# Where the weight sums of a decoder step are formed, and from which half of the work an input's block sums come

## The chip, the cores and the metric

The kernel is one launch on one core of a Trainium2 chip. The metric is device time in microseconds (us) for the whole launch, which is also how every span below is given. In the text PE is TensorE, DVE is VectorE, ACT is ScalarE, POOL is GpSimd and SP is SyncE; POOL and SP issue the DMAs here.

## The reference

A decoder step with one layer of mixer A, one shared projection of keys and values, and one layer of mixer B, on 1024 prompt tokens and 8 decoded ones, all in fp32, with 2048 channels:

```python
def pool_layer(x, prefix, pos, w_in, w_grp, scale, w_out, g_ln, b_ln):
    z = x @ w_in                                  # 2048 -> 4096
    u, gate = z[..., :D_POOL], z[..., D_POOL:]
    d, new_state = multiscale_pool(u, prefix, pos)
    d = jnp.einsum('btgc,gce->btge', d.reshape(B, T, 4, 512), w_grp)
    d = d.reshape(B, T, D_POOL) * scale
    y = (d * jax.nn.silu(gate)) @ w_out           # 2048 -> 2048
    return layer_norm(ALPHA * x + y, g_ln, b_ln), new_state

def attn_layer(x, ..., w_in, sinks, w_out, g_ln, b_ln):
    z = x @ w_in                                  # 2048 -> 4096
    q = rope_partial(z[..., :D_ATTN].reshape(B, T, N_HEADS, HEAD_DIM), pos)
    gate = z[..., D_ATTN:]
    o = attn_core(q, kb, vb, q_pos, k_pos, sinks).reshape(B, T, D_ATTN)
    y = (o * jax.nn.silu(gate)) @ w_out           # 2048 -> 2048
    return layer_norm(ALPHA * x + y, g_ln, b_ln)
```

`attn_core` is attention over a sliding window of 128 keys, with a sink per head.

## The kernel before, in words

**Stages.** The tokens are cut into chunk 0 (512) and chunk 1 (520, with the decoded tokens). Four matrix products (`wia`, `woa`, `wib`, `wob`) run one after the other, each for both chunks: ai0, ai1, ao0, ao1, bi0, bi1, bo0, bo1. These are the eight stages; the sixth is bi1, the seventh bo0 and the eighth bo1. bi also holds the attention, bo the last layer norm.

**Products.** Each matrix product is done by Strassen's scheme in Winograd's form: for each pair of output blocks (pairs 0 to 7 of a stage of 2048 outputs), seven block products in place of eight. They need sums of weight blocks and sums of input blocks. Every operand is split into a rounded part `hi` and a rest `lo`, so that a product is 24 matmuls (L687 hi·hi, L688 hi·lo, L689 lo·hi), some 2.8 us together. The products are counted from the start of the program; that count is the clock of the schedule (`self.i`). At the start of each product the program writes the weight loads that belong up to 7 products ahead (SP), the ACT cast of `hi` (L508) of 4 ahead, and the DVE subtraction for `lo` (L523) of 3 ahead. Every engine works in the order in which the source writes its instructions: an instruction that waits holds up all behind it on its engine.

**Sums of weights.** For `wob` they are formed in two ways. For most pairs `sum_gen` forms them ahead, in stages before bo0: one of four parts of a pair is loaded to a slot (two DMAs), added by DVE (L456 on 128x512, L460 and L461 on 128x256) and stored to DRAM by POOL (L462); bo0 and bo1 load the finished sums. It runs when the flag `on` is set and more than 5 slots are free. For pairs in `LATE` the sums are formed in bo0 itself, when they are first needed (`first_pair`: four DVE adds of 128x1024, L352, and four stores by POOL a pair, L354), and bo1 loads them.

**Sums of inputs.** `t_ops` makes the sums of an input's blocks: four DVE operations of 128x256 or 128x260 (L898 to L901), and a POOL store of 512 or 520 KB (L902, to a tensor named `to` for the input of bo). For the eighth stage `t_gen` does that in bo0, in eight steps that load, sum and store two rows of blocks of `o`; it is one of the side generators, of which a step is taken at products. When bo1's inputs are wanted, what is left of it is run at once.

**Slots.** All these buffers are 54 slots of SBUF (`Mem`); slot 14 shows as m14 in the rows of order below. A whole slot (`full`) is the one that has been free longest; a slot that was freed with a store under way counts as freed ten releases later than it was. `half` hands out half of a slot: the other half of one already broken up, unless that was freed within the last 6 releases and more than 7 whole slots are free. Nothing but the order of release keeps an instruction off a slot whose store isn't done; if it gets one, it waits for that store.

Of the kernel before, what the change touches and what calls it, by code (L numbers as in the profile page):

```python
# [69 lines left out]
    (6, 3), (7, 2), (7, 1), (6, 4), (7, 3), (7, 4), (4, 5), (4, 6), (5, 5), (5, 6), (6, 5), (6, 6), (7, 5), (7, 6),  # L70
)

LATE = (2, 3)
FORM = (0, 1)
X_KEEP = 5
X_AGE = 3
# [63 lines left out]
class Mem:  # L140
# [22 lines left out]
    def half(self, n=TMAX):  # L163
        fits = lambda i: i < NWIDE or n <= 512
        part = [
            (a if b is None else b, i) for i, (a, b) in enumerate(self.f) if (a is None) != (b is None) and fits(i)
        ]
        if part and min(part)[0] > self.clock - 6 and len(self.whole()) > 7:
            part = []
        i = min(part)[1] if part else min((i for i in self.whole() if fits(i)), key=lambda i: max(self.f[i]))  # L170
        h = 0 if self.f[i][0] is not None else 1
        if not part:
            self.new(i)
        self.f[i][h] = None
        w = TMAX if i < NWIDE else 512
        return Slot(self, i, h, self.t[i][:, h * w : (h + 1) * w])
# [15 lines left out]
class Kern:  # L192
# [187 lines left out]
    def build_stream(self):  # L380
        io = self.io
        w = []
        for kind, c, part in PHASES:
# [33 lines left out]
            else:  # L417
                name = "woa" if kind == "ao" else "wob"
                if (kind, c, part) != PHASES[-1]:
                    prs = [self.next_pair(name, q) for q in range(8)]  # L420
                    if (kind, c) == ("bo", 0):
                        for q in LATE:
                            prs[q] = self.first_pair(name, q)
# [10 lines left out]
    def sum_gen(self, name):  # L434


        W = 256
        qs = [q for q in range(8) if name != "wob" or q not in LATE]
        parts = [(q, slice(W * h, W * h + W)) for q in qs for h in range(4)]
# [144 lines left out]
    def both(self, c, P, Q):  # L584

        runs = [self.seven(c, z0, z1, {6: done}, own=own) for (z0, z1, done), own in (
            (P, self.psW), (Q, self.psW if self.wide else self.psO)
        )]
        for idx in ORDERL:
            for run in runs:  # L590
                run(idx)

    def pair(self, c, z0, z1, done, c11=None):

        run = self.seven(c, z0, z1, {6: done}, c11)
        for idx in ORDER7:
            run(idx)
# [304 lines left out]
        nc.gpsimd.dma_start(dst[:, kp], t)  # L902
        s.free(True)

    def t_gen(self, key):
        T = CHUNKS[key[1]][1]
        s = {}

        def load(kp):
            s[kp] = self.mem.full(2 * T)  # L910
            self.nc.sync.dma_start(s[kp].v(2, T), self.act[key][:, 2 * kp : 2 * kp + 2, :])

        load(0)
        yield
        for kp in range(9):
            if kp < 7:
                load(kp + 1)
            if kp:
                v = s[kp - 1].v(2, T)
                self.t_ops(v[:, 0], v[:, 1], self.Td[key], kp - 1, T // 2)  # L920
                s.pop(kp - 1).free()
            yield


    def j_steps(self, T, a, b, box, *free):
# [1357 lines left out]
    def run(self):  # L2283
        io = self.io
        self.build_stream()
        self.needs, self.pe, self.summed, self.hurry = [], {}, {}, None
        self.sg, self.qs, self.ao = {}, {}, {}
        self.last = self.turn = self.lock = False
        self.need = {}
        self.shared = False  # L2290
        self.strassen = False
        self.start()

        def add(key, gen):
            self.needs.append((key, gen))
            self.side.append(gen)

        acc, before = {}, False
        for n, (kind, c, part) in enumerate(PHASES):
            self.c, self.ph = c, kind + str(c)  # L2300
            self.strassen = (kind, c, part) not in PLAIN
            self.shared = False
            self.fresh = c == 1 and before and self.strassen
            before = c == 0 and self.strassen
            nxt = n + 1 if n + 1 < len(PHASES) else None
            self.every, self.room = 3, SIDE_KEEP
            if n == 0 or (kind, c) == ("bi", 0) and self.wide:
                self.use_four(kind == "ai")
            elif (kind, c) == ("bo", 0):
                self.at(18, lambda: self.use_four(True))  # L2310

            self.lock = (kind, c) in LOCKED
            self.need = {
                (idx, g): self.i + (2 * n + g - 1 if self.lock else n)
                for n, idx in enumerate(ORDERL if self.lock else ORDER7) for g in range(2)
            } if self.strassen else {}
            self.turn = not self.lock
            self.at(7, lambda: setattr(self, "turn", False))
            self.at(13, lambda: setattr(self, "lock", False))
            if n == 0:  # L2320
                self.at(10, lambda: self.x_begin(1))
                self.at(10, lambda: setattr(self, "turn", True))
            elif (kind, c) == ("ai", 0):
                add(("x", 1, False), self.t_gen(("x", 1)))
                self.room = 99
            elif (kind, c) == ("ai", 1):
                add(("g", 0, False), self.t_gen(("g", 0)))
                self.summed["woa"] = 0
                add("woa", self.sum_gen("woa"))
                self.every = 1.7  # L2330
            elif (kind, c) == ("ao", 0):
                self.every = 2
                self.at(1, lambda: self.nc.sync.dma_start(self.cst[:, K_MP:], io["mask"]))
            elif (kind, c) == ("ao", 1):
                gen = self.ln_gen(0, *acc[0], C_GA, C_BA, self.act["h", 0], self.Td["h", 0])
                self.at(3, lambda gen=gen: add(("h", 0, True), gen))
                self.every = 1.5
            elif (kind, c) == ("bi", 0) and not self.strassen:
                self.summed["wob"] = 0
                self.extra = self.sum_gen("wob")  # L2340
                for k in (4, 5):
                    self.at(k, lambda k=k: setattr(self, "on", k == 4))
                add(("h", 1, False), self.ln_gen(1, *acc[1], C_GA, C_BA, self.act["h", 1], self.Td.get(("h", 1))))

                for k in range(14):
                    self.at(2 * k + 5, lambda: self.side and self.lastO < self.i - 1 and self.side_step())
                self.every, self.room = 1, -20
            elif (kind, c) == ("bi", 1):
                self.at(8, lambda: setattr(self, "on", True))
                self.every, self.room = 1, 0  # L2350
            elif (kind, c) == ("bo", 0):
                self.at(23, lambda: setattr(self, "ahead", (7, 4, 3)))
                self.at(18, lambda: add(("o", 1, False), self.t_gen(("o", 1))))
                self.at(16, lambda: [s.free() for s in self.kv])
                self.rt.free()
            elif (kind, c) == ("bo", 1):
                gen = self.ln_gen(0, *acc[0], C_GB, C_BB, io["y0"], None)
                self.at(3, lambda gen=gen: add("y", gen))
                self.every, self.room = 1.5, 3
            if kind == "ai":  # L2360
                self.phase_ai(c, range(*part), nxt)
            elif kind == "bi":
                self.phase_bi(c, range(*part), nxt)
            else:
                res = self.act["x" if kind == "ao" else "h", c]
                last = (C_GB, C_BB, io["y1"]) if nxt is None else None
                acc[c] = self.phase_out(c, res, nxt, last)
# [141 lines left out]
```

## Time and profile before

| | us |
|---|---|
| three runs | 2311.48, 2312.7, 2317.13 (median 2312.7) |
| profiled execution | 2315.52, of which its span is 2313.7 |
| PE busy | 2285.5 (99% of the span) |
| DVE busy | 1904.7 (82%) |
| ACT busy | 1388.2 (60%) |
| POOL busy | 218.4 (9%) |

In the profiled execution bi0's Strassen products run from about 1217 us to 1504, bi1 to 1941, bo0 to 2128 and bo1 to the end. A row of the waits gives engine, tile and line that waited, what it waited for, us in total, times and the longest. A row of the windows gives a stretch, its length, each engine's busy time with its count of instructions, the mean clock that TensorE was granted (1.00 is full), the DMA engines' busy share and GB/s. A row of the timeline gives start, duration, engine, line, operation, destination and sources with their shapes, and the idle time ahead of it with what ended it. POOL's rows are DMA issues for the most part; the last number of a row of DMA issues is the median us from issue to landing.

### The profile page before, as it was taken

The page shows a single profiled execution, that of the slowest core. Times are in us where ns is not written, and L with a number is a line of the kernel's source. Part 1 is how long each engine was busy: PE and PEld are TensorE (multiplying, and loading weights), DVE is VectorE, ACT ScalarE, POOL GpSimd, SP SyncE. Part 2 cuts the span into 40 slices and gives each one's busy share as a digit, 9 for nine tenths or more (in the row PEclk, how much of TensorE's full clock was granted, in tenths as well). Part 3 has the DMA queues.
Part 4 walks back from the last instruction along what each step waited for, and adds up shares of the span by engine and source line. Part 5 has one row for each costly group of instructions (what it writes and reads, how often), then busy time and mean ns, then how long its engine had stood idle before and what let it go on. Part 6 is the DMA issues. An engine that isn't in the chain of part 4 may idle for free. (4 is left out here: it accounts for less than half of the span.)

```text
span 2313.7 us, 50523 instructions
## 1 busy us (share of the span) xinstructions
PE 2285.5 (99%) x20353; PEld 2214.5 (96%) x20353; DVE 1904.7 (82%) x2413; ACT 1388.2 (60%) x2551; POOL 218.4 (9%) x399
## 2 busy tenths in 40 slices
PE   9999999999999999999999999999999999899998
PEld 8999999999999999999889999999999999899998
DVE  8888889877878878988868888899776777788997
ACT  5544446444546556555567676785676678556665
POOL 0111110010000000000111111100010100010001
PEclk9999999999999999999999999999999999999999
DMA  7779679988889989999777767777776779699894
GB/s 259 266 263 316 228 249 330 314 305 301 301 305 322 338 286 331 320 385 343 236 249 238 243 225 251 268 264 234 242 247 224 250 238 315 210 359 363 297 333 150
DMA packets 252028, 647.77 MB, mean 280 GB/s; under 512 B 27504, under 2 KB 112528, under 8 KB 251792
## 3 DMA queue, kind: packets, MB, share of 16 engines
q1 hardware_dynamic: 208640, 490.20, 63.2%
q0 software_dynamic: 43152, 154.34, 17.3%
q8 instruction: 159, 2.61, 0.5%
q14 instruction: 77, 0.63, 0.1%
HBM read 467.21 MB, written 177.23 MB: 279 GB/s over the span
## 5 line engine op out<-in xcount | busy, mean ns | idle before, releaser
L687 PE MATMUL pD<-m,m 128*128 128x260 f32 (+1 forms) x5088 | 1443.6, 284 | 4.9 <-ACT pD L626 2.2
L689 PE MATMUL pD<-m,m 128*128 128x260 f32 (+1 forms) x5088 | 1436.2, 282 | 6.0 <-DVE m L523 5.7
L688 PE MATMUL pD<-m,m 128*128 128x260 f32 (+1 forms) x5088 | 1436.5, 282 | 0.0
L687 PEld LDWEIGHTS pD<-m,m 128*128 128x128 f32 x5088 | 960.7, 189 | 14.8 <-issue 7.2
L689 PEld LDWEIGHTS pD<-m,m 128*128 128x128 f32 x5088 | 961.4, 189 | 8.0 <-DVE m L523 8.0
L688 PEld LDWEIGHTS pD<-m,m 128*128 128x128 f32 x5088 | 960.8, 189 | 0.5
L523 DVE TENSOR_TENSOR m<-m,m 128x1024 fp32r<-128x1024 f32 x690 | 833.4, 1218 | 94.6 <-ACT m L508 32.2
L508 ACT CAST m<-m 128x1024 fp32r<-128x1024 f32 x690 | 720.6, 1049 | 231.6 <-DVE m L352 118.5
L352 DVE TENSOR_TENSOR m<-m,m 128x1024 f32<-128x1024 f32 x136 | 166.2, 1222 | 15.1 <-DMA m<-in_wia 10.4
L850 DVE TENSOR_TENSOR m<-m,m 128x1024 fp32r<-128x1024 f32 (+1 forms) x118 | 144.0, 1225 | 4.4 <-ACT m L841 3.8
L841 ACT CAST m<-m 128x1024 fp32r<-128x1024 f32 (+1 forms) x118 | 123.4, 1053 | 4.5 <-DMA m<-in_x 2.4
L648 DVE TENSOR_TENSOR m<-pD,m 128x260 f32<-128x260 f32 (+1 forms) x92 | 39.0, 424 | 101.4 <-ACT pD L647 95.3
L660 ACT COPY m<-pD 128x260 f32<-128x260 f32 (+1 forms) x88 | 32.8, 372 | 122.4 <-PE pD L689 121.8
L1935 ACT ACTIVATE m<-m,sm 128x128 f32<-128x128 f32 x256 | 99.3, 392 | 0.0
L632 ACT COPY m<-pD 128x260 f32<-128x260 f32 (+1 forms) x90 | 33.6, 373 | 97.8 <-PE pD L689 93.1
L1184 PE MATMUL pD<-m,m 128*128 128x260 f32 (+1 forms) x528 | 91.5, 323 | 0.0
L715 PE MATMUL pD<-m,m 128*128 128x512 f32 x224 | 89.0, 397 | 0.0
L635 ACT COPY m<-pD 128x260 f32<-128x260 f32 (+1 forms) x92 | 34.4, 374 | 90.8 <-PE pD L689 90.7
L717 PE MATMUL pD<-m,m 128*128 128x512 f32 x224 | 88.2, 394 | 0.0
L716 PE MATMUL pD<-m,m 128*128 128x512 f32 x224 | 88.2, 394 | 0.0
L1184 PEld LDWEIGHTS pD<-m,m 128*128 128x128 f32 x528 | 79.4, 188 | 8.2
L1948 ACT ACTIVATE m<-m,sm 128x128 f32<-128x128 f32 x256 | 81.9, 393 | 2.7 <-DVE sm L1943 2.5
(259 smaller groups left out, 2082.4 us busy)
## 6 DMA issues: line engine op xcount, KB each, us to landing
m<-in_wib SPq DMA_DIRECT2D x132, 512.0 KB
m<-in_wia SPq DMA_DIRECT2D x128, 512.0 KB
m<-swoa SPq DMA_DIRECT2D x64, 512.0 KB
swia<-m POOLq DMA_DIRECT2D x56, 512.0 KB, 4.6
m<-swia SPq DMA_DIRECT2D x56, 512.0 KB
m<-swob SPq DMA_DIRECT2D x56, 512.0 KB
m<-in_wob SPq DMA_DIRECT2D x52, 512.0 KB
m<-in_woa SPq DMA_DIRECT2D x48, 512.0 KB
```

What stands on the lines that cost most here:

```text
L352: self.nc.vector.tensor_add(s[out].a[:, :1024], s[x].a[:, :1024], s[y].a[:, :1024])
L508: self.nc.scalar.copy(hi.r[:, :1024], self.stream[self.cast].src().a[:, :1024])
L523: self.nc.vector.tensor_sub(lo.r[:, :1024], s.src().a[:, :1024], hi.a[:, :1024])
L687: nc.tensor.matmul(ps[:, :TH], wh[:, s], h, start=new and k == 0, stop=False, skip_group_check=on)
L688: nc.tensor.matmul(ps[:, :TH], wh[:, s], l, start=False, stop=False, skip_group_check=on)
L689: nc.tensor.matmul(ps[:, :TH], wl[:, s], h, start=False, stop=k == 7, skip_group_check=on)
L715: nc.tensor.matmul(ps[:], wh[:, s], h, start=par == 0 and k == 0, stop=False)
L716: nc.tensor.matmul(ps[:], wh[:, s], l, start=False, stop=False)
L841: self.nc.scalar.copy(h.r[:, :n], s.a[:, :n])
L850: self.nc.vector.tensor_sub(l.r[:, :n], s.a[:, :n], h.a[:, :n])
L1184: nc.tensor.matmul(ps[:, : cs.stop - cs.start], ws[:, s], d[:, cs], start=f0 and k == 0, stop=l0 and k == 3,)
L1935: nc.scalar.activation(x["s3"][:, i, :], x["s3"][:, i, :], AF.Exp, bias=nm[:, i : i + 1], scale=0.125, accum_out=rs[:, i : i + 1],)
```

## The change

Three things. `LATE` is empty, so that the sums of `wob` pairs 2 and 3 are formed by `sum_gen` too; for that `on` is set in bi0 as well, from its product 20 to 74. `t_gen` takes a range of steps: the first four rows of the eighth stage's input sums are made in bi1 (from its product 94), the other four in bo0. `half` breaks up a whole slot when more than 3 are free, where 7 were needed.

```diff
-LATE = (2, 3)
+LATE = ()
...
-        if part and min(part)[0] > self.clock - 6 and len(self.whole()) > 7:
+        if part and min(part)[0] > self.clock - 6 and len(self.whole()) > 3:
             part = []
...
-    def t_gen(self, key):
+    def t_gen(self, key, a=0, b=8):
...
-        load(0)
+        load(a)
         yield
-        for kp in range(9):
-            if kp < 7:
+        for kp in range(a, b + 1):
+            if kp < b - 1:
                 load(kp + 1)
-            if kp:
+            if kp > a:
...
             yield
+            if b < 8:
+                yield
+                yield
...
+            elif (kind, c) == ("bi", 0):
+                self.at(20, lambda: setattr(self, "on", True))
+                self.at(74, lambda: setattr(self, "on", False))
             elif (kind, c) == ("bi", 1):
+                self.at(94, lambda: add(("o", 1, False), self.t_gen(("o", 1), 0, 4)))
                 self.at(8, lambda: setattr(self, "on", True))
                 self.every, self.room = 1, 0
             elif (kind, c) == ("bo", 0):
                 self.at(23, lambda: setattr(self, "ahead", (7, 4, 3)))
-                self.at(18, lambda: add(("o", 1, False), self.t_gen(("o", 1))))
+                self.at(18, lambda: add(("o", 1, False), self.t_gen(("o", 1), 4)))
```

In the program as written out, bi0's products 422 to 476 hold ten parts of weight sums that were not there (30 DVE adds, 10 POOL stores, 20 SP loads), and between them 2 to 5 whole slots are free where 4 to 7 were. bi1 holds as many parts as before, of other pairs, and sixteen operations of `t_ops`. bo0 has lost eight adds of L352 with their eight POOL stores, and half of `t_gen`; pairs 2 and 3 load seven blocks each there and no longer five. Lines behind `t_gen` are 3 higher than before (L929 is now L932, L1986 is L1989).

The first place is on DVE, in bi0, where `t_ops` makes one row of the sums of bo0's input (in the trace of before at 1341 us). Before, the four operations fill slot m2, and the next `lo` goes to slot m21:

```order
L1986 SCALAR_TENSOR_TENSOR m50_1799_15736<-pO_281_15969,m14_1733_14883 128x512
L898 TENSOR_TENSOR m2_1823_16059<-m50_1799_15736 128x256
L899 TENSOR_TENSOR m2_1823_16059<-m50_1799_15736 128x256
L900 TENSOR_TENSOR m2_1823_16059<-m50_1799_15736,m2_1823_16059 128x256
L901 TENSOR_TENSOR m2_1823_16059<-m50_1799_15736,m2_1823_16059 128x256
L523 TENSOR_TENSOR m21_1828_16080<-m33_1801_15748,m1_1822_16028 128x1024
```

The same place now:

```order
L1989 SCALAR_TENSOR_TENSOR m42_1803_15754<-pO_281_15994,m45_1733_14883 128x512
L898 TENSOR_TENSOR m2_1828_16084<-m42_1803_15754 128x256
L899 TENSOR_TENSOR m2_1828_16084<-m42_1803_15754 128x256
L900 TENSOR_TENSOR m2_1828_16084<-m42_1803_15754,m2_1828_16084 128x256
L901 TENSOR_TENSOR m2_1828_16084<-m42_1803_15754,m2_1828_16084 128x256
L456 TENSOR_TENSOR m25_1817_15924<-m25_1817_15924 128x512
L523 TENSOR_TENSOR m2_1834_16107<-m14_1805_15766,m33_1827_16053 128x1024
```

The first add of a weight sum (L456) has come in, and the `lo` now writes into m2, the slot that POOL has just begun to store.

The second place is on DVE in bo0 (in the trace of before from 1991 us on): L929 adds up parts of the layer norm's sums into a half slot, and two lines later stand the last steps of the decoded tokens' attention (L2096 to L2098), which PE waits for. Before:

```order
L1986 SCALAR_TENSOR_TENSOR m23_2554_24310<-pS_215_13092,m31_2531_24123 128x512
L2085 COPY m23_2554_24310<-pS_215_13092 128x128
L2086 TENSOR_REDUCE sm_476_24311<-m23_2554_24310 128x1
L2087 SCALAR_TENSOR_TENSOR sm_476_24311<-sm_476_24311,prm_75 128x1
L2088 TENSOR_TENSOR sm_477_24312<-prm_75,sm_476_24311 128x1
L2089 TENSOR_SCALAR sm_476_24311<-sm_476_24311 128x1
L1344 SCALAR_TENSOR_TENSOR m39_2574_24464<-m42_2552_24305,m39_2574_24464 128x1024
L523 TENSOR_TENSOR m27_2634_24975<-m11_2621_24815,m26_2632_24929 128x1024
L929 TENSOR_TENSOR m23_2554_24310<-m39_2574_24464 128x512
```

The same place now:

```order
L1989 SCALAR_TENSOR_TENSOR m15_2582_24410<-pS_215_13092,m43_2559_24220 128x512
L2088 COPY m15_2582_24410<-pS_215_13092 128x128
L2089 TENSOR_REDUCE sm_476_24411<-m15_2582_24410 128x1
L2090 SCALAR_TENSOR_TENSOR sm_476_24411<-sm_476_24411,prm_75 128x1
L2091 TENSOR_TENSOR sm_477_24412<-prm_75,sm_476_24411 128x1
L2092 TENSOR_SCALAR sm_476_24411<-sm_476_24411 128x1
L1347 SCALAR_TENSOR_TENSOR m25_2602_24564<-m40_2580_24405,m25_2602_24564 128x1024
L523 TENSOR_TENSOR m32_2663_25071<-m52_2648_24913,m2_2660_25027 128x1024
L932 TENSOR_TENSOR m23_2665_25114<-m25_2602_24564 128x512
```

Before, L929 wrote into m23, a slot that L1986 had just filled in part with a block of `o` for POOL to store. Now L932 writes into a whole slot that has been free for long, not into m15.

## The prediction

> **What bounds the kernel now.** I read the head of the page first, then PE's waits over the span, then the stages that the change touches.
>
> ```profile
> PE 2285.5 (99%) x20353; PEld 2214.5 (96%) x20353; DVE 1904.7 (82%) x2413; ACT 1388.2 (60%) x2551; POOL 218.4 (9%) x399
> ```
>
> ```profile
> PE pD L689 <- DVE m L523: 5.7, 8, 2.2
> PE pS L2102 <- DVE m L2098: 5.3, 1, 5.3
> PE pD L687 <- ACT pD L626: 2.2, 2, 1.3
> PE pD L687 <- ACT m L660: 1.5, 2, 1.1
> ```
>
> PE is busy all but 28 us of 2313.7, and the change takes no matmul away. So it can win only where PE waits or runs at a lower clock, and can lose wherever DVE, ACT or a transfer comes late at a product. The two largest waits are for DVE. Most of them are in bo0:
>
> ```profile
> PE pS L2102 <- DVE m L2098: 5.3, 1, 5.3
> PE pD L689 <- DVE m L523: 2.5, 2, 2.2
> PE pD L687 <- ACT m L660: 1.5, 2, 1.1
> ```
>
> ```profile
> 1998.00:2009.00 11.00, 5.72 (x32) 5.52 (x30) 7.57 (x10) 3.23 (x5) 0.53 (x1) 0.69 0.32 112
> 2090.00:2094.00 4.00, 1.77 (x15) 1.57 (x14) 4.00 (x5) 1.24 (x2) 0.53 (x1) 1.00 1.04 405
> 2094.00:2098.00 4.00, 4.00 (x23) 4.00 (x22) 3.91 (x4) 3.40 (x6) 0.53 (x1) 0.57 1.05 408
> ```
>
> The first three rows are PE's waits between 1941 and 2128 us, the others windows. In 11 us from 1998, PE is busy 5.72 and the clock granted is 0.69; from 2090 it is idle 2.23 us, and the 4 us behind that run at 0.57. A wait costs more than its own length.
>
> **bo0: what the change removes.** DVE's timeline says why PE waited:
>
> ```profile
> 1994.27 1.22 DVE L523 TENSOR_TENSOR m<-m,m 128x1024 fp32r<-128x1024 f32 x1
> 2000.39 0.69 DVE L929 TENSOR_TENSOR m<-m 128x512 f32<-128x512 f32 x1 [4.91 <-DMA o<-m]
> ...
> 2088.73 0.43 DVE L898 TENSOR_TENSOR m<-m 128x260 f32<-128x260 f32 x1 [2.44 <-DMA m<-o]
> ```
>
> L929 waited 4.91 us for the store out of the slot that it was to write, with the attention steps L2096 to L2098 behind it. It now gets a slot long free, so this wait goes. The second wait is the rest of `t_gen`, run in one go when bo1's inputs are wanted: its L898 waited 2.44 us for a load of `o`. With half of the rows already made in bi1, the generator is done before that point, so this goes too. The 1.5 us for L660 stood behind ACT casts that waited for the L352 adds of pairs 2 and 3, and these are gone. In sum, against the profiled execution:
>
> - 1998 to 2009: idle 11.00 − 5.72 = 5.3, and for the clock up to 0.31 × 11 = 3.4; less if only PE's busy 5.72 us are counted as slowed (taken: 2.9).
> - 2090 to 2098: idle 2.2, clock 0.43 × 4 = 1.7.
> - L660: 1.5.
>
> That is 13.6 us. What could be late next is the load: pairs 2 and 3 load seven blocks and no longer five (2 MB more in all), and the DMA share is 1.04 around 2090. But POOL's eight stores of 512 KB (4 MB) leave the same stretch, and a part of `t_gen`'s loads and stores with them. I put the new lateness at 0, and keep 0 to 6 us.
>
> **bi1.** As many parts of sums are made as before, and 16 operations of `t_ops` come in, 16 × 0.43 = 6.9 us of DVE by this row:
>
> ```profile
> L901 DVE TENSOR_TENSOR m<-m,m x56: 424/428/432, 87.2 to 2089.9; 128x260 f32<-128x260 f32 x32, 128x256 f32<-128x256 f32 x24
> ...
> 1504.00:1941.00 437.00, 435.60 (x4756) 425.38 (x4756) 331.57 (x456) 302.12 (x708) 38.35 (x60) 1.00 0.75 246
> ```
>
> DVE has 437 − 332 = 105 us to spare there, so that is covered; without the cover it would be the 6.9. PE is idle 1.4 us in the stage, and later waits for loads may add a little: +0.5, between −1 and +4.
>
> **bi0: what the change adds.** This decides. The stretch that gets ten parts of sums, products 422 to 476, lies between 1291 and 1474 us:
>
> ```profile
> 1291.00:1474.00 183.00, 183.00 (x2072) 178.72 (x2072) 156.49 (x189) 130.17 (x320) 28.92 (x55) 1.00 0.68 237
> ...
> L456 DVE TENSOR_TENSOR m<-m x56: 653/684/691, 442.7 to 1900.3; 128x512 f32<-128x512 f32 x56
> L460 DVE TENSOR_TENSOR m<-m x56: 374/424/428, 443.4 to 1902.0; 128x256 f32<-128x256 f32 x56
> L461 DVE TENSOR_TENSOR m<-m x56: 424/426/428, 443.9 to 1902.5; 128x256 f32<-128x256 f32 x56
> ```
>
> PE never waits there. DVE is idle for 183 − 156.5 = 26.5 us. Ten parts take 10 × (0.68 + 0.42 + 0.43) = 15.3 us, some 14 because successive operations overlap a little. By itself that would fit. But the parts also hold slots, which leaves 2 to 5 free, and the one free longest is then often the one just given to POOL to store. In the order of the changed kernel, `lo` (L523) goes to such a slot six times between products 438 and 476: three times a slot of `t_ops` (m2, m14, m11), directly behind it or with one L456 between, and three times a slot of a weight sum (m25, m43, m2), one to five operations behind the store. Each L523 must wait until that store has landed, and with it all that DVE does next: other `lo`, the sums that ACT casts, the evacuation of PSUM. The trace of before shows such waits, and what stores take in bi0 and bi1:
>
> ```profile
> DVE m L929 <- DMA o<-m: 4.9, 1, 4.9
> DVE m L523 <- DMA swob<-m: 3.1, 1, 3.1
> ```
>
> ```profile
> swib<-m POOLq DMA_DIRECT2D x37, 512.0 KB, 3.2
> ...
> to<-m POOLq DMA_DIRECT2D x5, 512.0 KB, 6.7
> ...
> swob<-m POOLq DMA_DIRECT2D x23, 512.0 KB, 5.5
> ```
>
> A store of `to` took a median 6.7 us from issue to landing and one of `swob` 5.5; `swib`, whole slots without a stride, 3.2. With 0.5 us until POOL issues, a `lo` directly behind `t_ops` waits about 7 us, one behind L456 some 6, and those behind a weight sum 5.5 + 0.5 less the DVE work in between: 3.6, 1.7 and 4.8. Together 7 + 7 + 6 + 3.6 + 1.7 + 4.8 = 30 us.
>
> Why this reaches PE is seen at one such place. Before, there is no wait:
>
> ```profile
> 1341.83 0.42 DVE L901 TENSOR_TENSOR m<-m,m 128x256 f32<-128x256 f32 x1
> 1342.17 1.22 DVE L523 TENSOR_TENSOR m<-m,m 128x1024 fp32r<-128x1024 f32 x1
> ...
> 1346.41 1.23 DVE L523 TENSOR_TENSOR m<-m,m 128x1024 fp32r<-128x1024 f32 x1
> ```
>
> ```profile
> 1349.30 0.28 PE L689 MATMUL pD<-m,m 128*128 128x256 f32 x1
> ...
> 1352.13 0.28 PE L689 MATMUL pD<-m,m 128*128 128x256 f32 x1
> ```
>
> The `lo` that ends at 1343.39 is first used at 1349.30, 5.9 us later, the next (1347.64) at 1352.13, 4.5 later. That is all the lead DVE has. A wait of 6 us with an L456 ahead of it and two more adds of sums behind it (0.68 + 0.85) takes 7.5: the second of the two is then about 3 us late, and what is late on DVE stays so until it has idle time, of which there is 26.5 / 183 = 0.14 us in each us. Walked through the queue like this, the six places give PE waits of 5, 2, 4, 3, 6 and 2 us, 22 in all. A rougher count agrees: DVE is asked for 30 + 14 = 44 us more where it has 26.5, so at least 17.5 are left over. I take 20, and 3 more for clock, as waits of 2.2 and 5.3 us cost 1.7 and some 3 in the rows above. The lower bound goes by the `swib` row: if every store landed in 3.2 us, the six waits fall by 3 × 3.5 + 3 × 2.3 = 17 to some 13, the demand to 27, and DVE would just keep up: 0. The upper bound counts no idle time, only the lead of 4.5 twice: 30 + 14 − 9 = 35. Twenty is nearest to the rows of the same stores (6.7 and 5.5), so I keep those.
>
> The Trainium skill has a rule on these stores: in "DMA: Bandwidth & Descriptors", section "Anatomy of one DMA — SWDGE (gpsimd) path", a DMA of this path takes about 2.0 us and its bytes over 436 GB/s, which is 3.2 us for 512 KB, an estimate by that page. The `swib` row agrees with it and the `to` and `swob` rows don't, at 6.7 and 5.5 us; by the page's figure the loss in bi0 would be about none, which is the first rival below.
>
> The Trainium skill also says, in "TensorE: Matmul & The Clock Gate", section "HAM oscillation — how this bites in real kernels", that PE gaps of over some 3.4 us lower the clock. The window behind the 2.2 us gap, 0.57 for 4 us, shows that here a shorter one can do it as well; by the page only two or three of the six waits would cost clock.
>
> ACT and the queues: SP issues 20 more loads in bi0 and POOL ten more stores of 0.7 us issue time, with POOL busy 28.9 of 183 us, and DMA share 0.68. That adds 10 × 1 MB in 183 us to the row's 237 GB/s, about 57 more; the rows of bo0 show 405 GB/s, so I count it as hidden.
>
> **Sum.** −13.6 + 0.5 + 20 + 3 = +9.9 us. The profiled execution took 2315.5 (span 2313.7 and 1.8 around it), 2.8 above the median of 2312.7. Against the profile that is 2325.4; against the median 2322.6. I forecast 2322 on the median's scale.
>
> **The rivals.**
>
> - *Stores land early, or DVE catches up in its idle time* (faster). For it: the `swib` row of 3.2 us, the 26.5 us of idle time, and a DMA share of 0.68. The point that decides is the wait at `t_ops`: under about 4 us, the lead of 4.5 covers it. Then only bo0's gain is left: 2312.7 − 13.6 + 0.5 ≈ 2300. Against it: five stores of `to` in this stage at a median of 6.7. Chance 0.15.
> - *The two sides cancel* (no change). If the six waits hit singly, each with its lead restored, the loss in bi0 is 13 to 15 us: 2312 to 2316. For it: the places are some 10 to 28 us apart. Chance 0.2.
> - *The waits feed on each other* (slower). ACT's casts then come late too and PE falls to half clock after each gap: +31 in bi0 in place of 23, about 2331. For it: the clock rows. Chance 0.12.
> - *bo0's gain doesn't come*, since the two more blocks a pair arrive late in a stage where the DMA share reaches 1.04 (the change doesn't do what it says): 2312.7 + 23.5 ≈ 2336. Against it: 4 MB of stores leave. Chance 0.05.
>
> **How the numbers follow.** My forecast, 2316 to 2328 by itself, has 0.48. A measurement of this kernel tells 0.3% from no change, 6.9 us, so "slower" begins at 2319.6 and "faster" ends at 2305.8. Of the 0.48, 0.08 lies below 2319.6. Slower: 0.40 + 0.12 + 0.05 = 0.57; no change: 0.08 + 0.2 = 0.28; faster: 0.15. The range takes in the fastest case's 2300 and the slowest's 2336, and 2 us on each side for the spread of the runs (2311.5 to 2317.1 here): 2298 to 2338.
>
> **What would show it.** In the changed kernel's profile: waits of L523 for `to<-m` and `swob<-m` on DVE between 1291 and 1474 us, some 30 us in all, three of them 6 us or more; PE waits of L689 for L523 of about 20 us there, and a PEclk under 1 behind the longest; the end of bi0 some 23 us later than at 1504; then bo0 shorter by about 13, without the rows L2102 ← L2098 and DVE ← DMA `m<-o`. I am wrong if DVE's waits for these stores are under 4 us each, or if bo0 keeps its waits.

## The result, and the profile after

The changed kernel takes 2332.8 us (median of four runs, 2330.3 to 2338.4) against 2313.7 for the kernel before (four runs, 2311.5 to 2317.1): a ratio of 1.0085, 95% interval 1.007 to 1.0101. It is slower by 19 us, inside the forecast range (2298 to 2338) and of the forecast sign, by twice the forecast amount. The profiled execution of the changed kernel is the fastest of its four, at 2330.3 with a span of 2328.5, so the two profiles differ by 14.8 us, and not by 19.

The windows are cut at the first product of each stage: bi0, bi1 and bo0 of the kernel after, then bi0 and bo0 of before.

```profile
1217.00:1533.00 316.00, 295.57 (x3221) 284.00 (x3219) 256.30 (x329) 202.89 (x481) 53.62 (x98) 0.98 0.73 254
1533.00:1970.00 437.00, 435.39 (x4756) 425.16 (x4756) 336.06 (x467) 302.48 (x707) 39.14 (x62) 1.00 0.76 252
1970.00:2143.00 173.00, 172.74 (x1596) 170.91 (x1596) 141.52 (x167) 113.71 (x196) 7.56 (x14) 1.00 0.87 301
```

```profile
1217.20:1504.40 287.20, 286.52 (x3221) 278.98 (x3219) 245.92 (x301) 204.31 (x483) 46.22 (x88) 1.00 0.71 246
...
1941.00:2128.00 187.00, 177.95 (x1597) 175.28 (x1598) 156.80 (x191) 114.19 (x196) 13.95 (x26) 0.97 0.87 312
```

With the first products to a tenth, bi0 went from 287.2 to 316.0 (+28.8), bi1 from 436.6 to 436.7, bo0 from 187.2 to 173.6 (−13.6), bo1 by −0.2 and what stands before bi0 by −0.3. In bo0 PE is now busy all but 0.3 us; in bi0 it is idle 316.0 − 295.6 = 20.4 us, where it was idle 0.7. PE's largest waits in bi0, then DVE's, then ACT's, and last ACT's wait for L523 in the kernel before:

```profile
PE pD L687 <- ACT m L635: 6.5, 4, 2.3
PE pD L689 <- DVE m L523: 4.8, 5, 1.7
PE pD L687 <- ACT pD L647: 4.7, 4, 2.1
```

```profile
DVE m L523 <- DMA to<-m: 14.0, 2, 7.4
DVE m L523 <- DMA swob<-m: 10.5, 3, 5.0
DVE m L523 <- ACT m L635: 7.4, 1, 7.4
...
ACT m L508 <- DVE m L523: 29.3, 12, 6.2
ACT m L508 <- DVE m L352: 23.7, 13, 3.1
ACT m L508 <- DMA o<-m: 15.8, 3, 5.7
...
ACT m L508 <- DVE m L523: 6.1, 7, 1.3
```

DVE waits 31.9 us at L523, at six places, for slots whose store had not landed. One of the six is put down to L635. That is a case of a wait for several things, where the name is of the one that seems to come last: the `lo` there writes into m14, which `t_ops` had just filled, its store was issued at 1402.6 us and landed 7.0 us later, and the wait ends then. It is the third wait for a store of `to`. PE waits for ACT more than for DVE, and the six places show two ways in which this comes about. The first of the three places with a store of `to` shows one of them (DVE's timeline, then ACT's):

```profile
1342.63 0.43 DVE L901 TENSOR_TENSOR m<-m,m 128x256 f32<-128x256 f32 x1
1342.97 0.68 DVE L456 TENSOR_TENSOR m<-m 128x512 f32<-128x512 f32 x1
1350.30 1.22 DVE L523 TENSOR_TENSOR m<-m,m 128x1024 fp32r<-128x1024 f32 x1 [6.64 <-DMA to<-m]
...
1343.29 0.37 ACT L632 COPY m<-pD 128x256 f32<-128x256 f32 x1 [1.37 <-PE pD L689]
1348.83 1.04 ACT L508 CAST m<-m 128x1024 fp32r<-128x1024 f32 x1 [5.17 <-DMA o<-m]
1349.79 0.37 ACT L635 COPY m<-pD 128x256 f32<-128x256 f32 x1
```

At the same time ACT's cast (L508) waits 5.17 us for another store, that of a block of `o`, and L635, which empties a PSUM bank for PE, stands behind it. So both engines that feed PE are held at once. The other way is seen at the three places where the store is one of `swob` (DVE, ACT and PE at one of them):

```profile
1380.35 1.23 DVE L523 TENSOR_TENSOR m<-m,m 128x1024 fp32r<-128x1024 f32 x1 [3.55 <-DMA swob<-m]
...
1381.61 1.04 ACT L508 CAST m<-m 128x1024 fp32r<-128x1024 f32 x1 [6.14 <-DVE m L523]
...
1382.98 0.39 PE L687 MATMUL pD<-m,m 128*128 128x256 f32 x1 [2.29 <-ACT m L635]
```

Here DVE alone waits for a store; ACT's cast waits for that `lo`, and L635 (at the other two places L647, another copy that PE waits for) stands behind the cast. Windows of 20 us show the clock:

```profile
1384.00:1404.00 20.00, 20.00 (x226) 19.45 (x225) 17.42 (x26) 13.87 (x37) 4.28 (x8) 0.91 0.67 238
1404.00:1424.00 20.00, 17.75 (x134) 17.11 (x133) 14.09 (x20) 8.34 (x25) 3.10 (x5) 0.91 0.51 168
```

### The profile page after: what moved, and what is told of

Same layout as the page of the kernel before. It is cut to its first block, busy times and chain, and to the rows that moved or that the text cites. A ratio compares the mean times of both kernels' runs of the same rounds, so it can differ in the third digit from the quotient of the medians.

```text
span 2328.5 us, 50598 instructions
## 1 busy us (share of the span) xinstructions
PE 2289.8 (98%) x20353; PEld 2215.5 (95%) x20353; DVE 1904.2 (82%) x2429; ACT 1386.9 (60%) x2551; POOL 220.4 (9%) x399
## 4 chain that ended last, share of the span: by engine, by line
PE 45%; DVE 5%; issue 4%; DMA 2%; ACT 2%; POOL 0%; DVEq 0%; SPq 0%; POOLq 0%; ACTq 0%
PE pD L687 12%; PE pD L689 12%; PE pD L688 11%; PE pD L715 2%; PE pD L717 2%; PE pD L716 2%; DVE m L523 2%; PE pO L1980 2%; PE pS L1902 1%; DVE m L352 1%; PE pS L1955 1%; DMA swob<-m 1%; DMA to<-m 1%; ACT m L508 0%; PE pS L1980 0%
## 5 line engine op out<-in xcount | busy, mean ns | idle before, releaser
L689 PE MATMUL pD<-m,m 128*128 128x260 f32 (+1 forms) x5088 | 1435.9, 282 | 8.0 <-DVE m L523 7.8
L689 PEld LDWEIGHTS pD<-m,m 128*128 128x128 f32 x5088 | 960.8, 189 | 10.7 <-DVE m L523 10.7
L523 DVE TENSOR_TENSOR m<-m,m 128x1024 fp32r<-128x1024 f32 x690 | 832.4, 1217 | 112.8 <-ACT m L508 31.9
L508 ACT CAST m<-m 128x1024 fp32r<-128x1024 f32 x690 | 720.2, 1048 | 269.0 <-DVE m L352 110.7
L352 DVE TENSOR_TENSOR m<-m,m 128x1024 f32<-128x1024 f32 x128 | 156.4, 1222 | 17.9 <-DMA m<-in_wia 11.8
L635 ACT COPY m<-pD 128x260 f32<-128x260 f32 (+1 forms) x92 | 34.4, 374 | 83.3 <-PE pD L689 83.0
```

The costliest lines, as they stand in the source:

```text
L352: self.nc.vector.tensor_add(s[out].a[:, :1024], s[x].a[:, :1024], s[y].a[:, :1024])
L508: self.nc.scalar.copy(hi.r[:, :1024], self.stream[self.cast].src().a[:, :1024])
L523: self.nc.vector.tensor_sub(lo.r[:, :1024], s.src().a[:, :1024], hi.a[:, :1024])
L689: nc.tensor.matmul(ps[:, :TH], wl[:, s], h, start=False, stop=k == 7, skip_group_check=on)
```

## The experiments

All runs change the kernel before or the changed one by a few lines; `...` stands for code that stays. Each is judged by its stages, cut as above, and by its time where it was run several times against the kernel before; a stage's time is that of one execution, and in the runs that leave bi0 untouched it takes 286.9 to 287.2 us. **Theory A**: bi0 is longer since slots run short and instructions get slots whose store is under way. **Theory B**: bi0 is longer since the thirty adds are too much for DVE.

**Two slots taken away in bi0 of the kernel before, and nothing else**

```diff
             elif (kind, c) == ("bo", 0):
...
+            elif (kind, c) == ("bi", 0):
+                box = []
+                self.at(20, lambda: box.extend(self.mem.full(1024) for _ in range(2)))
+                self.at(74, lambda: [s.free() for s in box])
```

> The kernel before, with nothing of the change, but two slots are taken from the pool during bi0's products 20 to 74 and left unused. No sum is added. In its order three L523 write into the slot that t_ops has just given to POOL to store, and three ACT casts (L508) into the slot of a block of o just given to POOL. Theory A (slots run short, so DVE and ACT wait for stores under way): waits of L523 for to<-m of some 7 us, three of them, waits of L508 for o<-m of 4 to 6 us, and bi0 longer by 8 to 15 us (each wait of 7 less the lead of 4.5, and as much again for ACT and the clock). Theory B (the thirty adds are too much for DVE): bi0 as before, within 1 us. Elsewhere as before in both.

bi0 took 296.1 us, 8.9 more, with no add, load or store added. The window of bi0, DVE's waits and ACT's there:

```profile
1216.50:1512.60 296.10, 289.50 (x3221) 279.38 (x3219) 243.40 (x299) 204.16 (x484) 46.37 (x88) 1.00 0.69 236
```

```profile
DVE m L523 <- ACT m L635: 12.5, 2, 6.8
...
DVE m L523 <- DMA to<-m: 5.6, 1, 5.6
...
ACT m L508 <- DMA o<-m: 8.9, 3, 3.7
```

Three L523 wait 18.1 us in all, under two names, and three casts 8.9 us: the six of the order. bi0 is longer by what theory A gave, though the casts wait less than it gave (3.7 us at the longest). A scarce slot alone makes bi0 slower. Both engines wait at the same time here too (ACT, then DVE, at the first of the three places):

```profile
1347.05 1.05 ACT L508 CAST m<-m 128x1024 fp32r<-128x1024 f32 x1 [3.66 <-DMA o<-m]
...
1348.46 1.23 DVE L523 TENSOR_TENSOR m<-m,m 128x1024 fp32r<-128x1024 f32 x1 [6.78 <-ACT m L635]
```

**The thirty adds alone**

```diff
+            elif (kind, c) == ("bi", 0):
+                for k in range(10):
+                    self.at(22 + 5 * k, lambda: self.work(0))    # one add of 128x448
+                    self.at(23 + 5 * k, lambda: self.work(1))    # two adds of 128x256
```

> The kernel before, with thirty adds more on DVE in bi0 (ten times one of 128x448 and two of 128x256, some 14 us), at products five apart from 22 on, in the unused part of a slot that is held anyway: no slot, load or store is added and the sums of weights are made as before. Theory A: DVE's 26.5 us of idle time take them in, bi0 within 1.5 us of before. Theory B: bi0 longer by 10 us or more.

```profile
1216.60:1503.70 287.10, 286.42 (x3220) 278.86 (x3219) 257.35 (x330) 203.85 (x483) 46.22 (x88) 1.00 0.71 246
```

DVE is busy 257.4 us in bi0, more than in the changed kernel (256.3), and bi0 takes what it took before. Theory B falls.

**Both at once**

> The kernel before with both edits at once: two slots taken away in bi0's products 20 to 74, and the thirty adds in the unused part of a held slot. The first alone cost bi0 8.9 us, the second nothing. If the two only add up, bi0 is 9 us longer than 287. Theory A says more: the adds use up the idle time in which DVE catches up after a wait for a store, so bi0 is 13 to 20 us longer, with the same six waits.

bi0 took 299.3 us, 12.1 more than before, with waits of the same kind (11.3 us of L523 under the name of `to<-m`, 9.2 of L508 for `o<-m`). The adds that cost nothing by themselves cost 3 us beside the waits, as they would if they use up idle time in which DVE would catch up. The interaction is there, but smaller than the 13 to 20 us that I expected.

**The changed kernel without parts in bi0**, in two forms: pairs 2 and 3 put back into bo0 (`LATE = (2, 3)`), or all parts made from bi1 on (`LATE` empty).

```diff
-            elif (kind, c) == ("bi", 0):
-                self.at(20, lambda: setattr(self, "on", True))
-                self.at(74, lambda: setattr(self, "on", False))
```

> The changed kernel with the sums of pairs 2 and 3 put back into bo0 and none made in bi0; the split of t_gen and the rule of half are kept. Theory A and B: bi0 as before (287). bo0: the two long waits (L2102 for L2098, and L898 for its load) are gone, the 1.5 us for L660 may stay: 175 where the change has 173.6 and before has 187. Total some 12 us under before (about 2301). Rival: the gain in bo0 comes from the eight adds and stores that were taken away there; then bo0 stays above 183.

> The changed kernel without the window in bi0: the ten parts are made in bi1 with the others, everything else as changed. Theory A: bi0 as before (287), bo0 as in the change (173.6); bi1 gets 14 us of adds into 105 us of idle time, but more slots are taken there, so between 0 and 5 us longer than 436.7. Total 8 to 13 us under before. Theory B says the same of bi0, and up to 14 us more in bi1.

Both missed: 2314.2 us against 2313.1 (ratio 1.0003, 0.9994 to 1.0013), and 2311.9 (0.9995, 0.9986 to 1.0004). bi0 was 287.0 and 286.9, as expected. But bi1 grew by 3 to 5 us, and bo0 stayed at 182.2 and 179.9. The two long waits in bo0 are gone there, and others have come at its start. PE's waits in bo0 with pairs 2 and 3 put back, and the window of its first 20 us:

```profile
PE pD L687 <- ACT pD L626: 2.2, 1, 2.2
PE pD L687 <- ACT m L641: 1.8, 1, 1.8
PE pD L687 <- ACT m L660: 1.5, 2, 1.1
```

```profile
1943.00:1963.00 20.00, 15.61 (x136) 14.98 (x121) 16.11 (x20) 16.06 (x38) 1.29 (x2) 0.96 1.04 362
```

In these programs the sums of weights run on to product 618 and 650, past bo0's start at 612; in the kernel before they end at 603, in the changed one at 611. So the parts in bi0 did have a use in the change: they made room for the sixteen operations of `t_gen` in bi1.

**The sums alone**: the kernel before with `LATE` empty and the window in bi0, the rule of `half` and `t_gen` as before.

> The kernel before with pairs 2 and 3 formed ahead (LATE empty) and the window in bi0, without the split of t_gen and with the old rule of half. In its order it is ACT's cast (L508), and no L523, that writes into slots just given to POOL in bi0 (ten within two products). Theory A: ACT has more lead, but L523 waits for the cast; bi0 longer by 5 to 20 us, with waits of L508 for to<-m and swob<-m. bo0: L929 (a half of a slot just given to POOL) and the burst of t_ops are as before, so bo0 loses only what the eight adds and stores cost, 0 to 5 us under 187.

This one had two surprises. The windows are bi0 and bo0, the waits ACT's in bi0 and DVE's in bo0:

```profile
1216.90:1512.80 295.90, 288.64 (x3221) 279.19 (x3219) 259.17 (x335) 202.82 (x482) 55.25 (x100) 1.00 0.81 278
...
1947.40:2123.00 175.60, 174.04 (x1607) 171.76 (x1600) 145.57 (x180) 113.05 (x196) 9.74 (x18) 1.00 0.89 317
```

```profile
ACT m L508 <- DMA to<-m: 14.5, 3, 6.3
...
DVE m L929 <- DMA o<-m: 2.0, 1, 2.0
```

bi0 is longer by 8.7 us only, although twelve parts are made there, two more than in the change: the old rule breaks up 8 whole slots in these products, where the new one breaks up 14. And bo0 is at 175.6 with the old rule of `half` and the whole of `t_gen`: without the eight adds and stores L929 waits 2.0 us where it waited 4.91, and the load that L898 waited for comes in time. I had expected at most 5 us there. This gave **theory C**: most of the loss in bi0 comes from the new rule of `half` together with the parts.

**The change with the rule of `half` as it was**

```diff
-        if part and min(part)[0] > self.clock - 6 and len(self.whole()) > 3:
+        if part and min(part)[0] > self.clock - 6 and len(self.whole()) > 7:
```

> The changed kernel with one number put back: half breaks up a whole slot only when more than 7 are free. The ten parts in bi0 and their adds, loads and stores stay as in the change. In its order no L523 in bi0 gets a slot just given to POOL; the casts (L508) do. Theory C (most of the loss in bi0 comes from the rule of half together with the parts: whole slots broken up where few are left, so that L523 and L508 both wait for stores): bi0 294 to 298 where the change has 316, as in the run with the sums only (295.9). Theory A as I first had it (the parts alone take the slots): bi0 stays above 310. bo0 172 to 176, total 2306 to 2312 by theory C.

```profile
1216.30:1513.60 297.30, 289.68 (x3221) 280.66 (x3219) 259.59 (x335) 202.40 (x482) 55.09 (x100) 0.99 0.80 277
1948.20:2121.80 173.60, 173.59 (x1605) 171.95 (x1601) 140.24 (x165) 112.75 (x196) 7.59 (x14) 1.00 0.87 300
```

2309.2 us against 2313.1 (ratio 0.9984, 0.9975 to 0.9993), where the change is at 1.0085: one number is worth some 23 us. bi0 is 297.3 and bo0 173.6. Contrary to what I expected, the parts don't stay as they were: twelve are made in bi0, where the change makes ten, so bi0 is shorter with more work and more traffic in it (277 GB/s in this window, 254 in that of the change). That also bounds a rival that no run takes alone, the added DMA traffic: together with the adds and what the old rule leaves of the waits, it costs at most the 10 us by which bi0 is longer than before. The same place as above shows the mechanism (DVE's timeline, then ACT's):

```profile
1342.46 0.68 DVE L456 TENSOR_TENSOR m<-m 128x512 f32<-128x512 f32 x1
1343.06 1.22 DVE L523 TENSOR_TENSOR m<-m,m 128x1024 fp32r<-128x1024 f32 x1
...
1347.65 1.05 ACT L508 CAST m<-m 128x1024 fp32r<-128x1024 f32 x1 [4.62 <-DMA to<-m]
```

It is now the cast alone that gets the slot of `to`; L523 goes on at once. With the new rule `half` breaks up one more whole slot there, so that the cast gets the slot of `o` and L523 the next one, that of `to`. At this place one engine waits with the old rule, and both with the new one. In the whole of bi0 no L523 waits for a store with the old rule, and six do with the new one.

**The rule of `half` alone, and the split of `t_gen` alone**, each in the kernel before

> The kernel before with the new rule of half alone. Theory C: without the parts it costs bi0 nothing (287). bo0: L929 gets a slot long free, so the wait of L2102 for L2098 and the low clock behind it go (8 us by my sum); the burst of t_ops at 2090 stays: bo0 178 to 181, total 5 to 9 us under before.

> The kernel before with the split of t_gen alone (LATE and the rule of half as before). bo0: the wait of L898 for its load and the clock behind it go (3.9 us by my sum), the wait of L2102 stays at 5: bo0 180 to 184. bi1, where sixteen operations come in and its sums of weights run on to about product 618: 437 to 441. Total within 4 us of before.

The windows are bi0 and bo0 with the rule of `half`, then bo0 with the split:

```profile
1215.80:1502.70 286.90, 286.27 (x3220) 278.70 (x3218) 246.57 (x301) 203.63 (x483) 46.23 (x88) 1.00 0.72 246
...
1938.20:2116.20 178.00, 174.35 (x1607) 171.82 (x1601) 156.68 (x191) 113.97 (x197) 13.95 (x26) 1.00 0.91 329
```

```profile
1946.90:2129.60 182.70, 176.22 (x1608) 174.04 (x1601) 151.93 (x177) 113.31 (x197) 12.48 (x23) 0.98 0.85 299
```

The rule alone makes the kernel faster: 2305.5 against 2313.1 (0.9967, 0.9955 to 0.998), with bi0 untouched. So the edit that costs most in the change is the one that gains most by itself; what it meets in bi0 decides. The split alone moves nothing (2314.6, ratio 1.0005, 0.9996 to 1.0015): bo0 falls to 182.7, and bi1 grows to 441.3.

**Fewer parts in bi0, in the gaps**: the changed kernel with pairs 2 and 3 (then pair 3 only) in bo0, and four parts in bi0

```diff
-                self.at(20, lambda: setattr(self, "on", True))
-                self.at(74, lambda: setattr(self, "on", False))
+                for p in ((28, 29), (42, 43), (56, 57), (70, 71)):
+                    self.at(p[0], lambda: setattr(self, "on", True))
+                    self.at(p[1], lambda: setattr(self, "on", False))
```

> The changed kernel with pairs 2 and 3 put back into bo0, and in bi0 only four parts, each begun in the gap between two steps of t_ops (flag set for one product at 28, 42, 56 and 70), so that no L523 gets a slot within two products of its store there. The other parts then end at product 602 of the program, where they ended at 618 with none made in bi0. Theory A: bi0 287 to 288. bo0 175 (without the waits at its start, where sums of weights ran on before), bi1 436.5 to 439: total 9 to 13 us under before. Rival: the split of t_gen by itself delays bo0's start; then bo0 stays at 182 and the total is within 3 us of before.

> As the run with four parts, but only pair 3 stays in bo0 and pair 2 is formed ahead, so that the parts run on to product 618. If sums that run into bo0's start are what gave back the gain there, bo0 starts with waits as with none made in bi0 (some 4 us and clock) and takes about 180; total 5 to 9 us under before, above the run with four parts.

```profile
1216.70:1504.90 288.20, 286.81 (x3220) 279.02 (x3219) 249.29 (x311) 203.70 (x483) 49.33 (x92) 1.00 0.76 257
1504.90:1940.50 435.60, 434.55 (x4755) 424.83 (x4753) 334.99 (x462) 303.61 (x708) 37.73 (x60) 1.00 0.76 248
1940.50:2116.50 176.00, 174.00 (x1603) 171.75 (x1600) 150.13 (x174) 113.20 (x196) 11.86 (x22) 1.00 0.87 308
```

2304.5 us against 2313.8 (ratio 0.9961, 0.9947 to 0.9974), better than both kernels: bi0 288.2, as the four parts end before `t_ops` needs its slot, and bo0 176.0, since the sums end at product 602. With pair 2 formed ahead the sums end at 618 again, PE waits 3.5 us at its longest for L626, and the gain is 5.5 us (2308.2, 0.9977, 0.9968 to 0.9986). Both came out close to what I expected, and the pair of them bears out that sums which run into bo0 give its gain back.

**The rule of `half`, four parts, one pair ahead, `t_gen` whole**

> The kernel before with the new rule of half, pair 2 formed ahead, and four parts in bi0 in the gaps between the steps of t_ops; pair 3 stays in bo0 and t_gen isn't split. Sums end at product 607 (603 before, 611 in the change). Theory C: bi0 288 (four parts in the gaps, as measured), bi1 436 to 437, bo0 175 to 178 (four adds and four stores fewer than with the rule of half alone, 178.0; the burst of t_ops may still cost 2). Total 2302 to 2306, at or just under the run with the rule of half alone (2305.5) and the one with four parts (2304.5).

2304.0 us against 2313.6 (0.9961, 0.9947 to 0.9974), bi0 288.4, bi1 435.7, bo0 175.2. It can't be told from the run with four parts, and it is 1.5 us under the rule of `half` alone, whose runs spread over 3.4 us; the split of `t_gen` isn't needed.

## Why the prediction was right, and where it was off

**bo0, −13.6.** It came out at −13.6: the two waits and the low clock behind them are gone, and PE is idle 0.3 us. I had put 5.3 + 2.9 down to the slot of L929, 3.9 to the split and 1.5 to the adds. Alone, the rule of `half` brings 9.2 (187.2 to 178.0) and the split 4.5, close to these shares; the sums formed ahead bring 11.6, and there my 1.5 was wrong, since without the eight adds and stores both long waits nearly go as well. That is 25 in all: the edits in part remove the same waits. The kernel before itself had bo0 between 185 and 187 in runs that leave it untouched, so these shares hold to about 2 us.

**bi1, +0.5.** It was +0.1. In bi1 the changed kernel makes 21 parts of sums where the kernel before makes 23, and not as many as before, as I had it. What I had not seen is that the forecast depends on the parts made in bi0: without them (`LATE` empty), bi1 takes 4.8 us and bo0 6.3 us more than in the change.

**bi0, waits of 30 us on DVE and 20 us of idle PE.** Measured: 31.9 us at the six places (21.4 for stores of `to`, where I had 20, and 10.5 for stores of `swob`, where I had 10.1), and PE idle 19.7 us more than before. The stores took what I had taken (in bi0 of the changed kernel, issue to landing):

```profile
swob<-m POOLq DMA_DIRECT2D x10, 512.0 KB, 5.1
to<-m POOLq DMA_DIRECT2D x6, 512.0 KB, 6.9
o<-m POOLq DMA_DIRECT2D x11, 256.0 KB, 6.5
```

With these the page of the Trainium skill that I weighed, "DMA: Bandwidth & Descriptors", section "Anatomy of one DMA — SWDGE (gpsimd) path", disagrees: its fit gives an estimate of 3.2 us for 512 KB, and `to` takes twice that.

That the sum for idle PE agreed is in part luck. I had forecast PE waits of 5, 2, 4, 3, 6 and 2 us at the six places, 22 in all, of L689 for L523. In order of time they came out at 3.9, 2.1, 2.3, 2.0, 2.0 and 2.8, 15 in all; another 3.6 us are waits of the attention (L1980), which I had not counted. And L689 waits for L523 only 4.8 us. Most of the rest passes through ACT, at three places behind casts that waited for stores of `o` (15.8 us of ACT), at the other three behind casts that waited for a late `lo`; ACT's waits for L523 grew from 6.1 to 29.3 us.

That casts come late and the clock falls was my rival *the waits feed on each other*, with a chance of 0.12, +31 in bi0 and about 2331 in all. The measured 28.8 and 2332.8 lie nearer to it than to my own 23 and 2322, so my range held, but the rival was the better forecast. It lacked that casts wait for stores of their own, and the clock falls at three places only.

Two engines that wait at once aren't by themselves what makes bi0 dear: in the run with the two slots taken away both wait at the same three places, and bi0 loses 8.9 us. With the old rule of `half` put back, the casts alone wait (16.4 us for stores of `to` and `swob`), and bi0 loses 10. The changed kernel has the three places with both engines, longer waits there, three more places with stores of `swob`, and the adds. What each of these is worth in the 28.8 no run separates.

**bi0, clock 3 us.** This is the term that was mis-sized. Beside the idle time, the same matmuls are busy 295.6 us where they were 286.5, 9 us more. Windows of 4 us show the clock low at three places (the third goes on to 1476 at 0.85):

```profile
1384.00:1388.00 4.00, 4.00 (x23) 4.00 (x22) 3.93 (x7) 2.66 (x11) 0.00 (x0) 0.57 0.02 5
1412.00:1416.00 4.00, 4.00 (x24) 4.00 (x23) 3.83 (x8) 2.01 (x10) 0.00 (x0) 0.60 0.02 4
1468.00:1472.00 4.00, 3.49 (x21) 3.49 (x22) 3.90 (x6) 0.62 (x4) 0.00 (x0) 0.73 0.05 22
```

That is 4 × (0.43 + 0.40 + 0.27 + 0.15) = 5 us for the clock. Some 3 of the other 4 us are waits that the table of busy time hides, by an estimate: the last matmuls before the wait at 1382.98 start at 1380.29 and 1380.41, 0.12 us apart, and each counts as busy for 0.28, so each of the 19 waits that are new hides some 0.16 us. The rest I can't separate. The clock fell behind a gap of 2.3 us, behind 1.1 and 0.9 close together, and behind 1.8 and 1.0; behind gaps of 2.1 (at 1362 us) and 2.0 (at 1447) it stayed at 1.00. On this the Trainium skill's page "TensorE: Matmul & The Clock Gate", section "HAM oscillation — how this bites in real kernels", says that it takes gaps of over some 3.4 us; PE's longest single wait in bi0 is 2.3 us, so here shorter ones did it, though not each of them.

**The cause.** The step "the parts also hold slots" was right, but took the parts for the whole of it. It is parts and rule together: with the parts (twelve of them) and the old rule bi0 is 296 to 297, with the rule and no parts 287, with both 316. That the two together make the loss is shown; how they do it is seen in the order and in the waits, but its pieces weren't tried one by one.

**The total.** 20 + 3 became 28.8, which makes 14.8 us for the profiled executions where I had 9.9. The other 4 us between that and the medians are spread of executions: the profiled one was the fastest of the changed kernel, and 2 us above the median of the kernel before.

## What to carry to other kernels

A pool that hands out the buffer longest free hides its stores only while there are enough buffers: count the free ones at the place where most are held, and look in the order for an instruction that writes into a buffer whose store was issued a moment ago. Work that fits into an engine's idle time can still cost through the buffers it holds; here thirty adds were free, and two buffers cost 9 us. Try each edit of a change alone and left out: the rule that cost 23 us inside this change gains 7.5 us by itself.

## What was not expected of the hardware

PE's clock can fall after short gaps: no wait in bi0 of the changed kernel exceeds 2.3 us by the table of waits, and the 4 us behind the one of 2.3 us ran at 0.57. Not each gap does it: in the run with the sums alone the clock stayed at 1.00 behind one of 2.5 us, and with the old rule of `half` put back it fell to 0.50 behind one of 2.8. And a DMA store of 512 KB by POOL took 5.1 us (`swob`), 6.9 us (`to`) or 3.2 to 5.5 us (`swib`) in the same stage of different kernels: the size alone does not give its time.
